# Hybrid attention and recurrent layer on one core: six gate columns as three two-column units of seven half-products in the recurrent stage, and new owners for two small jobs of the attention stage

## The chip, the cores and the metric

The kernel runs on one core of one Trainium2 chip. The metric is device time in microseconds (us); of several runs the median is told. One further execution was recorded by the hardware profiler, and all rows below come from it. The engines are PE (TensorE: matrix products and transposes), DVE (VectorE), ACT (ScalarE), POOL (GpSimd) and SP (SyncE, which here only issues transfers). Each works through its own queue in order, and waits for the others by semaphores.

## The reference, cut to what matters

One layer for 1024 prompt frames and 32 decode frames, 1056 columns in the kernel:

```python
h = _rms_norm(x, g_pre_mix)
z = h @ w_in
qa, ka, va, qb, fb, ib, ob, ga, gb = jnp.split(z, SPLIT_POINTS, axis=-1)
...
ya = _sink_attention(...)             # 16 heads of width 64, 2 kv heads
yb, s_fin = _hgrn2(qb, fb, ib, s0, lb, block)    # 8 heads of width 128
mix = jax.nn.sigmoid(ga) * (ya @ w_br_a) + jax.nn.sigmoid(gb) * (yb @ w_br_b)
x = x + _rms_norm(mix @ w_out, g_post_mix)
...                                   # ConvFFN and the per-layer input
```

Everything is float32. The two gates `ga` and `gb` are 1024 wide each: 16 gate columns of 128. They depend on `h` and `w_in` alone and are needed first in the mix, so the kernel can compute them whenever it likes before that.

## The kernel before, in words

**Products.** Activations lie transposed, 128 rows of features by frames. A float32 product is made of three products of rounded halves: every operand is split into a high part (a copy into a rounding type) and a low part (the value less the high part), and `product` (L195) issues high x high (L200), high x low (L201) and low x high (L202). The frames are three groups `GR` of 384, 384 and 288 columns. A weight column of 128 outputs has eight blocks of 128 inputs, so a plain column is 3 groups x 8 blocks x 3 = 72 products: 48 on 384 columns and 24 on 288. `La`, `Lb` are the high and low parts of `h`.

**Weights.** `plan` lists the weight columns in the order of their use. `load_raw` (L168) issues the load on SP into one of two `wr` buffers. `load_next` (L173) makes the two halves in the eight `wb` buffers: the high half on ACT (L181) or, from position 28 of the attention stage on, on DVE (L183, switched by `hi_on`), the low half on DVE (L184). `next_w` keeps two columns ahead of the one in use.

**Attention stage** (L841 to L875). `stream` (L256) runs 18 plain columns as blocks of 24 products (one group of one column), two halves of 12 each: eight q columns (the first begun earlier), eight columns of `ga` and three of `gb` (`GB_AT`). After each half it runs small jobs listed for that position. For each of eight pairs of heads i and nine tiles of frames j these are `scores` (four products on PE, L451 and L452; addition of the bias and minimum on DVE, L457; exp on ACT, L462; reciprocal and two scalings on DVE, L464 and L466; the sink's column on POOL, L455), `turn` (four transposes on PE, L478; high half `ph` on ACT, L223; low half `pl` on DVE, L224) and `values` (products on PE, L500 and L501; two copies on ACT, L507; two additions on DVE, L509). `turn` stands three halves behind `scores`, `values` two behind `turn`. The gates' products are there because the small jobs load DVE and ACT more than PE. `h_sums` (L514) makes sums of quarters of `h` on DVE, for the next stage, and stores them through POOL's queue (L528, to `t_d`); `ya` is stored when a pair is done.

**Recurrent stage** (L878 to L1318). One more plain gate column bridges the change of stage. Then the 32 columns of q, f, i and og run as 16 units of two columns. A unit (`unit_pieces`, L991) computes the 384-column groups 0 and 1 of two columns together in the seven block products of Strassen's scheme (Winograd's form): seven pieces of 12 products on 384 columns, in place of eight. Group 2 stays plain, four pieces of 12 on 288 columns. Operands are quarters of `h` or their sums (`TH`, `TL`, loaded from `t_d` at L885, split by `t_split` at L887), and quarters of the weights or their sums (`b_parts`, L922: eight splits, L931 on ACT and L932 on DVE, and four sums on DVE, L933 to L944). The bias of the scheme is settled in the evictions e0 to e10: copies on ACT, additions on DVE. In between run the small jobs of the recurrence (decay, factors, turns, `tile_in`, `tile_out`, `group_out`). After head 7 the last four gate columns follow as plain blocks: `tail[:8]` still beside head 7's jobs, `tail[8:]` beside `load_split` of `ya` (L1337: load on SP into `ld`, split into `Ra` on ACT and `Rb` on DVE), which feeds the next stage's products (`Ra`, L1379).

**Order.** PE, DVE and ACT queues are ordered by the framework's scheduler from the program above; `pinned`, `step` and `behind` fix a few jobs. Each queue is then executed in order.

## Time and profile before

| what | value |
|---|---|
| median of 3 runs | 2001.58 us (2001.55 to 2002.27) |
| the profiled execution's own time | 2002.58 us |
| its span, first to last instruction | 2000.8 us |
| PE busy | 1984.3 us (99%) |
| DVE, ACT, POOL busy | 71%, 48%, 11% |
| attention stage, scores of the first pair to the last values | 56.5 to 372.8 us |
| recurrent stage with the tail, to the first product on `Ra` | 385.8 to 871.6 us |

The profiled execution is 1.00 us above the median; its time is 1.78 us more than its span. A row of a group gives line, engine, operation, output and inputs, form and count, then the busy time and the mean of one in ns, then the idle time of the engine just before and what ended it. A matmul's duration in a row contains its fill and drain, and overlaps with the next one; the pace of matmuls is the distance of their starts. Instructions on DVE and ACT overlap a little as well, so the busy time of a stretch is less than the sum of its durations.

### The profile page before, as it was taken

What the parts mean: (1) busy time and instruction counts of PE and PEld (TensorE: products, weight loads), DVE (VectorE), ACT (ScalarE), POOL (GpSimd) and SP (SyncE); (2) the same over time, 40 slices, a digit from 0 to 9 for tenths busy, and PEclk for the clock granted to TensorE, in tenths of its full rate; (3) what the DMA queues carried; (4) which work ended last, traced back from release to release, by engine and by line L of the source; (5) the groups of instructions that cost most, each with busy time, mean ns of one, the idle gap of its engine ahead of it and who ended that gap; (6) DMA issues with size and microseconds to landing.
All of it is one profiled execution on the core that took longest, in us unless ns stands there. A gap on an engine that the chain in (4) does not pass through costs nothing.

```text
span 2000.8 us, 37359 instructions
## 1 busy us (share of the span) xinstructions
PE 1984.3 (99%) x14304; PEld 1955.0 (98%) x14304; DVE 1424.5 (71%) x3138; ACT 965.4 (48%) x2159; POOL 228.4 (11%) x323
## 2 busy tenths in 40 slices
PE   8999999999999999999999999999999999999998
PEld 7899999999999999999999999999999999999998
DVE  6788888688888888554455788788888784655552
ACT  7555566566666666442124663333333344444432
POOL 1110100000000000002001023333333210000000
PEclk9999999999999999999999999999999999999999
DMA  7622311411111111377558582222222245655543
GB/s 257 155 92 85 106 53 55 154 43 58 58 37 51 41 54 54 123 241 220 166 165 291 173 288 70 80 76 86 76 86 76 86 141 195 213 192 173 171 130 80
DMA packets 253639, 247.47 MB, mean 124 GB/s; under 512 B 13893, under 2 KB 221912, under 8 KB 253461
## 3 DMA queue, kind: packets, MB, share of 16 engines
q1 hardware_dynamic: 245141, 218.59, 35.3%
q0 software_dynamic: 8240, 26.44, 3.7%
q8 instruction: 112, 1.84, 0.4%
q14 instruction: 66, 0.54, 0.1%
q10 hardware_dynamic: 80, 0.07, 0.0%
HBM read 177.56 MB, written 65.32 MB: 121 GB/s over the span
## 4 chain that ended last, share of the span: by engine, by line
PE 92%; DVE 4%; ACT 2%; DMA 1%; issue 1%; POOL 0%; SPq 0%; DVEq 0%; ACTq 0%; POOLq 0%
PE mm L200 14%; PE mm L201 14%; PE mm L202 14%; PE st L1867 7%; PE st L1866 7%; PE st L1865 7%; PE G L1009 2%; PE Y L1006 2%; PE G L1008 2%; PE G L1006 2%; PE Y L1009 2%; PE Y L1008 2%; PE tr L478 1%; PE X L1006 1%; PE so L1200 1%; PE X L1009 1%
## 5 line engine op out<-in xcount | busy, mean ns | idle before, releaser
L1865 PE MATMUL st<-op,wt 128*128 128x264 f32 x1232 | 348.6, 283 | 2.0 <-DVE Sp L1878 1.3
L1867 PE MATMUL st<-op,wt 128*128 128x264 f32 x1232 | 349.8, 284 | 0.0
L1866 PE MATMUL st<-op,wt 128*128 128x264 f32 x1232 | 347.6, 282 | 0.0
L184 DVE TENSOR_TENSOR wl<-wr,wh 128x1024 fp32r<-128x1024 f32 x129 | 157.9, 1224 | 120.7 <-ACT wh L181 111.7
L1865 PEld LDWEIGHTS st<-op,wt 128*128 128x128 f32 x1232 | 231.2, 188 | 3.5 <-DVE Sp L1878 1.7
L1866 PEld LDWEIGHTS st<-op,wt 128*128 128x128 f32 x1232 | 231.4, 188 | 0.0
L1867 PEld LDWEIGHTS st<-op,wt 128*128 128x128 f32 x1232 | 230.9, 187 | 0.0
L181 ACT CAST wh<-wr 128x1024 fp32r<-128x1024 f32 x116 | 121.8, 1050 | 197.7 <-PE mm L201 136.1
L200 PE MATMUL mm<-La,wh 128*128 128x384 f32 (+1 forms) x528 | 174.4, 331 | 0.0
L201 PE MATMUL mm<-Lb,wh 128*128 128x384 f32 (+1 forms) x528 | 170.9, 324 | 0.6 <-DVE Lb L710 0.6
L200 PE MATMUL mm<-ac,wh 128*128 128x352 f32 x528 | 170.8, 323 | 0.0
L202 PE MATMUL mm<-La,wl 128*128 128x384 f32 (+1 forms) x528 | 170.5, 323 | 0.2 <-DVE wl L685 0.2
L202 PE MATMUL mm<-ac,wl 128*128 128x352 f32 x528 | 169.8, 322 | 0.0
L201 PE MATMUL mm<-ac,wh 128*128 128x352 f32 x528 | 169.3, 321 | 0.0
L1625 ACT CAST wt<-wu 128x512 fp32r<-128x512 f32 x126 | 77.9, 619 | 186.6 <-POOL ab L1851 88.3
L200 PE MATMUL mm<-Ra,wh 128*128 128x264 f32 x512 | 145.4, 284 | 0.0
L201 PE MATMUL mm<-Rb,wh 128*128 128x264 f32 x512 | 145.0, 283 | 0.0
L202 PE MATMUL mm<-Ra,wl 128*128 128x264 f32 x512 | 145.0, 283 | 0.0
L1626 DVE TENSOR_TENSOR wt<-wu,wt 128x512 fp32r<-128x512 f32 x126 | 103.0, 820 | 39.0 <-ACT wt L1625 39.0
L462 ACT ACTIVATE sc<-sc,st 128x257 f32<-128x257 f32 (+1 forms) x144 | 69.7, 485 | 74.0 <-DVE st L457 73.0
L201 PEld LDWEIGHTS mm<-Lb,wh 128*128 128x128 f32 x528 | 99.4, 188 | 1.7 <-DVE Lb L710 1.4
L202 PEld LDWEIGHTS mm<-La,wl 128*128 128x128 f32 x528 | 99.2, 188 | 0.7 <-DVE wl L685 0.5
(496 smaller groups left out, 5694.8 us busy)
## 6 DMA issues: line engine op xcount, KB each, us to landing
wr<-in_w_down_dram SPq DMA_DIRECT2D x66, 512.0 KB
wu<-in_w_up_dram SPq DMA_DIRECT2D x42, 512.0 KB
wu<-in_w_in_dram SPq DMA_DIRECT2D x32, 512.0 KB
wr<-in_w_in_dram SPq DMA_DIRECT2D x25, 512.0 KB
ac<-act_d SPq DMA_DIRECT2D x66, 176.0 KB
act_d<-Up SPq DMA_DIRECT2D x21, 528.0 KB
wr<-in_w_out_dram SPq DMA_DIRECT2D x16, 512.0 KB
pw_d<-pw POOLq DMA_DIRECT2D x11, 512.0 KB, 5.6
```

Source lines behind the costliest of these rows:

```text
L181: S.copy(hi[:], raw[:])
L184: V.tensor_tensor(lo[:], raw[:], hi[:].bitcast(F32), op=ALU.subtract)
L200: E.matmul(ps, wh, a, start=first and n == 0, stop=False)
L201: E.matmul(ps, wh, b, start=False, stop=False)
L202: E.matmul(ps, wl, a, start=False, stop=last and n == len(ks) - 1)
L1006: E.matmul(o, wh, x[0][k], start=first and k == 0, stop=False, skip_group_check=True)
L1008: E.matmul(o, wh, x[1][k], start=False, stop=False, skip_group_check=True)
L1009: E.matmul(o, wl, x[0][k], start=False, stop=k == 3, skip_group_check=True)
L1626: V.tensor_tensor(t[:, 1], src, t[:, 0].bitcast(F32), op=ALU.subtract)
L1865: E.matmul(o, wh, xh, start=first and k == 0, stop=False, skip_group_check=True)
L1866: E.matmul(o, wh, xl, start=False, stop=False, skip_group_check=True)
L1867: E.matmul(o, wl, xh, start=False, stop=k == 3, skip_group_check=True)
```

## The change

- **Where the gates are computed.** The 16 gate columns are one list `GATES`, all of `ga` first. The attention stage gets 21 blocks, seven columns (before: eleven), spread by `G_AT` over the eight pairs: 6, 2, 2, 2, 2, 2, 2, 3. A pair from the second to the seventh has five blocks where it had six (the fourth had nine), and the last has three where it had six. One plain column still bridges the stages. Six columns become three units of two columns in the recurrent stage, after heads 2, 5 and 7 (`gate_unit`, `G_AFTER`), each of 11 pieces. Two plain columns are left for the tail: three of their six blocks beside head 7's last jobs, three beside `load_split`.
- **Low halves of weights in attention.** From position 28 on ACT makes the high half and also writes the negated value, rounded, into the low half's tile; a transfer issued from POOL then adds the raw weight to it in place (`accum_op`).
- **Scaling.** Of the two heads of a tile DVE scales one, ACT the other.
- **Order.** `h_sums` is cut into four steps, for pairs 1, 2, 4 and 5 (before: two whole at pair 0, two at pair 3). `values` stands three halves behind `turn`. At the end `back` (which reloads a part of `h` that was overwritten) comes after the last piece in place of the third last, since the gate unit's sum `gu` lies in the same buffer. Units use the `wr` and `wb` buffers alternately, counted from the end.

```diff
+    GATES = [(ta_d[c], 5376 + c * P) for c in range(8)] + [(tb_d[c], 6400 + c * P) for c in range(8)]
+    G_AT = (6,2,2,2,2,2,2,3)
+    N_A = sum(G_AT) // 3
...
-        if hi_on[0] == "act":
-            S.copy(hi[:], raw[:])
+        S.copy(hi[:], raw[:])
+        if lo_by[0] == "vector":
+            V.tensor_tensor(lo[:], raw[:], hi[:].bitcast(F32), op=ALU.subtract)
         else:
-            V.tensor_copy(hi[:], raw[:])
-        V.tensor_tensor(lo[:], raw[:], hi[:].bitcast(F32), op=ALU.subtract)
+            S.mul(lo[:], raw[:], -1.0)
+            gdma(lo[:], raw[:], accum_op=ALU.add)
...
-            for h in range(2):
-                V.tensor_scalar(sc[:m_, h, b0:e_], sc[:m_, h, b0:e_], st[:m_, 1, h:h + 1], None,
-                                op0=ALU.mult)
+            V.tensor_scalar(sc[:m_, 0, b0:e_], sc[:m_, 0, b0:e_], st[:m_, 1, 0:1], None, op0=ALU.mult)
+            S.mul(sc[:m_, 1, b0:e_], sc[:m_, 1, b0:e_], st[:m_, 1, 1:2])
...
+        H_AT = (1, 2, 4, 5)
+        of_gates = [b for n in range(N_A) for b in unit(gate_out(GATES[n][0]))]
         for i in range(8):
             lo_ = 2 * len(blocks) if i else 0
-            blocks += unit(gate_out(ta_d[i]))
-            if i in GB_AT:
-                blocks += unit(gate_out(tb_d[GB_AT.index(i)]))
-            if i < 7:
-                blocks += unit(q_out(i + 1))
-            hi_ = 2 * len(blocks) - (6 if i == 7 else 0)
+            q = unit(q_out(i + 1)) if i < 7 else []
+            g = [of_gates.pop(0) for _ in range(G_AT[i])]
+            blocks += g + q if i == 0 else q + g
+            hi_ = 2 * len(blocks) - (4 if i == 7 else 0)
...
-                    small.setdefault(at + 5, []).append(lambda i=i, js=js: values(i, js))
+                    small.setdefault(at + 6, []).append(lambda i=i, js=js: values(i, js))
...
+    G_AFTER = {2: N_A + 1, 5: N_A + 3, 7: N_A + 5}
+    BU, unit_at = [], {}
     for h in range(8):
+        unit_at[h] = len(BU)
         BU += [(1280 + h * P, 2304 + h * P), (3328 + h * P, 4352 + h * P)]
+        if h in G_AFTER:
+            BU.append(tuple(GATES[G_AFTER[h] + a][1] for a in range(2)))
...
-        cb = lp.tile([P, T], F32, tag="Lb10", name="cb")
+        cb_gu = lp.tile([P, T + GMAX], F32, tag="Lb10", name="cb")
+        cb, gu = cb_gu[:, 0:T], cb_gu[:, T:T + GMAX]
...
+        def gate_unit(h):
+            def out(dst):
+                def f(g, src):
+                    o, n = GR[g]
+                    t = gtile()
+                    S.activation(t[:, :n], src, AF.Tanh, scale=0.5)
+                    dma(dst[:, o:o + n], t[:, :n])
+                return f
+            a, b = (out(GATES[G_AFTER[h] + i][0]) for i in range(2))
+            return unit_pieces(unit_at[h] + 2, lambda: gu, a,
+                               lambda g: bt("x0", GMAX, 1)[:], b)
...
             pieces += qf_unit(h) + io_unit(h)
             m1 = m0 + NP
+            if h in G_AFTER:
+                pieces += gate_unit(h)
...
-        at(len(pieces) - 3, back)
+        at(len(pieces) - 1, back)
...
-        for c in range(4, 8):
-            u = unit(gate_out(tb_d[c]))
-            tail += [u[0], u[2], u[1]]
-        stream(tail[:8], {m - len(pieces): f for m, f in small.items()})
+        u, v = (unit(gate_out(dst)) for dst, _ in GATES[14:])
+        tail = [u[0], u[2], v[0], v[2], u[1], v[1]]
+        stream(tail[:3], {m - len(pieces): f for m, f in small.items()})
...
-        stream(tail[8:], small)
+        stream(tail[3:], small)
```

What the scheduler makes of it on ACT, a stretch inside one pair of the attention stage, before (`sc` are scores, `st` their statistics, `ph` a turned high half, `gt` a gate, `u` and `o` values, `qa` and `qb` queries):

```order
L462 ACTIVATE sc_3258,st_3259<-sc_3258,st_3259 128x257 x2
L292 ACTIVATE gt_3280<-mm_3234 128x384
L507 COPY u_3288<-o_3283 64x32
L508 COPY u_3288<-o_3283 64x32
L223 CAST ph_3294<-tr_3296 128x256
L223 CAST ph_3314<-tr_3316 128x512
L462 ACTIVATE sc_3328,st_3329<-sc_3328,st_3329 128x257
L292 ACTIVATE gt_3350<-mm_3301 128x288
L462 ACTIVATE sc_3328,st_3329<-sc_3328,st_3329 128x257
```

and the same engine in a pair of the changed kernel that makes two weight columns:

```order
L465 ACTIVATE sc_2701,st_2702<-sc_2701,st_2702 128x257 x2
L182 CAST wh_2920<-wr_2918 128x1024
L469 ACTIVATE sc_2701<-sc_2701,st_2702 128x256
L413 ACTIVATE qa_2723<-mm_2663 64x288
L226 CAST ph_2731<-tr_2733 128x512
L465 ACTIVATE sc_2745,st_2746<-sc_2745,st_2746 128x257
L416 ACTIVATE qb_2724<-mm_2663 64x288
L465 ACTIVATE sc_2745,st_2746<-sc_2745,st_2746 128x257
L226 CAST ph_2768<-tr_2770 128x512
L186 ACTIVATE wl_2921<-wr_2918 128x1024
L469 ACTIVATE sc_2745<-sc_2745,st_2746 128x256
```

New in ACT's queue are the cast of the high half (L182), the negated copy (L186) and, behind each tile's two exps, the scaling (L469), which needs DVE's reciprocal of what these exps have summed.

At the end of the attention stage SP's queue reads before:

```order
L293 DMA tb_d_111<-gt_5014 128x384
L512 DMA ya_d_92<-ya_4194 128x1056
L293 DMA tb_d_111<-gt_5067 128x288
L885 DMA TL_5076<-t_d_128 128x1536
L885 DMA TL_5079<-t_d_129 128x1536
```

and now:

```order
L514 DMA ya_d_92<-ya_3970 128x1056
L296 DMA ta_d_108<-gt_4803 128x384
L896 DMA TL_4725<-t_d_128 128x1536
L896 DMA TL_4728<-t_d_129 128x1536
```

The loads of the sums of `h` still stand behind the store of the last `ya` and one store of a gate. On PE, though, the last values product is now followed by 7 products on 384 columns and 24 on 288 before the recurrent stage's first pieces; before, it was 48 on 384 and 35 on 288.

At the end of the recurrent stage SP's queue reads now (the stores `yb_d` are head 7's last outputs, `ld` the loads that feed `Ra`):

```order
L1288 DMA yb_d_100<-sg_10334 128x384
L296 DMA tb_d_115<-gt_10828 128x288
L1288 DMA yb_d_100<-sg_10259 128x384
L296 DMA tb_d_116<-gt_10868 128x384
L1288 DMA yb_d_100<-sg_10349 128x288
L1370 DMA ld_10906<-ya_d_85 128x264
L1370 DMA ld_10910<-ya_d_86 128x264
```

As before, the first load stands right behind the last output of head 7. On PE that output's transposes were followed by 72 products on 384 columns and 24 on 288 before the first product on `Ra`; now it is 48 and 24.

More of the change, by code (lines that the diff above doesn't have):

```diff
@@ L860, in layer_kernel @@
                     small.setdefault(m, []).append(lambda: pinned(load_next, S, V))
[L861 removed]
+                small.setdefault(28, []).append(lambda: lo_by.__setitem__(0, "dma"))
             if i < 7:
                 small.setdefault(lo_ + 2, []).insert(0, lambda i=i: bias_load(i + 1))
[L864 to L865 removed]
+            if i in H_AT:
+                sums = h_sums(H_AT.index(i))
+                next(sums)
+                for m in range(4):
+                    small.setdefault(lo_ + 2 * m + 1, []).append(
+                        lambda sums=sums: pinned(lambda: next(sums), V))
             for j in range(9):
```

49 lines of the change are left out of this document (25 added, 24 removed).

## The prediction

> **What bounds the kernel now.** I read the page first: the shares of the engines, then the chain of waits.
>
> ```profile
> span 2000.8 us, 37359 instructions
> PE 1984.3 (99%) x14304; PEld 1955.0 (98%) x14304; DVE 1424.5 (71%) x3138; ACT 965.4 (48%) x2159; POOL 228.4 (11%) x323
> PE 92%; DVE 4%; ACT 2%; DMA 1%; issue 1%; POOL 0%; SPq 0%; DVEq 0%; ACTq 0%; POOLq 0%
> ```
>
> PE is busy nearly throughout and owns 92% of the chain. "Busy" may hide a PE that only creeps, so next I read starts, at a place with nothing but products (the timeline of PE):
>
> ```profile
> 864.21 0.29 PE L200 MATMUL G<-La,wh 128*128 128x288 f32 x1
> 867.39 0.34 PE L200 MATMUL X<-La,wh 128*128 128x384 f32 x1
> 871.56 0.28 PE L200 MATMUL mm<-Ra,wh 128*128 128x264 f32 x1
> 871.92 0.29 PE L200 MATMUL mm<-Ra,wh 128*128 128x264 f32 x1
> ```
>
> Between the first two starts lie 24 products on 288 columns: 3.18/24 = 0.1325 us each. Between the second and the third lie 24 on 384: 4.17/24 = 0.174 us. Three on 264 take 0.36 us. Then the stages that the change touches, in windows: the second, the sixth and the last pair of heads of the attention stage, and one head of the recurrent stage (54.74 us):
>
> ```profile
> core 0: us, PE busy (x) PEld busy (x) DVE busy (x) ACT busy (x) POOL busy (x), PEclk, DMA share, GB/s
> 115.10:149.00 33.90, 33.90 (x239) 33.67 (x237) 29.81 (x95) 20.10 (x63) 4.22 (x16) 1.00 0.29 95
> 266.60:301.90 35.30, 35.30 (x250) 34.80 (x249) 29.09 (x94) 21.11 (x66) 2.35 (x13) 1.00 0.21 69
> 337.30:372.80 35.50, 34.64 (x245) 33.32 (x244) 25.01 (x90) 20.93 (x67) 1.58 (x8) 1.00 0.12 42
> 500.00:554.74 54.74, 54.74 (x362) 53.19 (x362) 46.50 (x132) 34.68 (x93) 0.00 (x0) 1.00 0.18 53
> ```
>
> PE has no idle time in three of these, at a granted clock of 1.00. The sixth pair has six blocks, two columns: 2 x (48 x 0.174 + 24 x 0.1325) = 23.1 us of its 35.3 us. The other 12.2 us are the small jobs' own products and transposes. So PE bounds both stages, and only fewer products, or a new wait, move the time.
>
> **The saving.** Three units compute six columns with seven block products where eight stood, on groups 0 and 1: three pieces of 12 products on 384 columns fewer, 36 x 0.174 = **6.25 us**. All other products of the gates are only moved. In the recurrent stage a gate unit takes PE 84 x 0.174 + 48 x 0.1325 = 21.0 us and brings DVE eight splits, four sums and five evictions:
>
> ```profile
> L932 DVE TENSOR_TENSOR wt<-wu,wt 128x512 fp32r<-128x512 f32 x12 | 8.1, 685 | 1.8 <-ACT wt L931 1.7
> L1027 DVE TENSOR_TENSOR x<-s1c,Y 128x384 f32<-128x384 f32 x1 | 0.6, 554 | 0.3 <-PE Y L1009 0.3
> ```
>
> 12 x 0.685 + 5 x 0.554 = 11.0 us, 52% of 21.0, where a head has 46.5/54.74 = 85%. The unit thins DVE's load, and PE covers it. I count it at nothing; without that cover it would cost up to 11 us a unit. It also follows head 7, where DVE is crowded; the row of PE's idle time there,
>
> ```profile
> L1232 PE MATMUL so<-vk,am 128*128 128x128 f32 x16 | 3.3, 287 | 0.5 <-DVE S L1210 0.5
> ```
>
> is a wait for DVE that the plain tail could not avoid. With the start's delay I put it at 0.7 us and take it as gone (bounds 0 and 0.7): **-0.7 us**.
>
> **Attention, ACT and DVE.** A pair loses one block of six, on average 23.1/6 = 3.9 us, so PE needs 31.4 us. ACT's additions, by these rows of the pair at 266.6 (the first from the page):
>
> ```profile
> L181 ACT CAST wh<-wr 128x1024 fp32r<-128x1024 f32 x116 | 121.8, 1050 | 197.7 <-PE mm L201 136.1
> L462 ACT ACTIVATE sc<-sc,st 128x257 f32<-128x257 f32 x14 | 7.1, 507 | 6.6 <-DVE st L457 6.6
> L223 ACT CAST ph<-tr 128x256 fp32r<-128x256 f32 x1 | 0.4, 373 | 0.0
> ```
>
> The trace has no scaling on ACT. Its nearest rows are 0.373 us (a cast of as many columns) and 0.507 us (an exp with a per-row scale and a sum); I take 0.42, since there is no sum: nine make 3.8 us (3.4 to 4.6). A weight column costs two passes, 2 x 1.05 = 2.1 us; by the new order of ACT the third, fourth and sixth pairs make two columns, the second and fifth one, the seventh none. ACT goes from 21.1 us to 21.1 - 0.45 (a gate's tanh) + 3.8 + 4.2 = 28.65 us of 31.4 (91%) in the heavy pairs, 26.5 or 24.4 in the others. DVE by rows of the same pair:
>
> ```profile
> L184 DVE TENSOR_TENSOR wl<-wr,wh 128x1024 fp32r<-128x1024 f32 x3 | 3.7, 1226 | 0.2
> L183 DVE CAST wh<-wr 128x1024 fp32r<-128x1024 f32 x2 | 1.4, 688 | 0.0
> L466 DVE TENSOR_SCALAR sc<-sc,st 128x256 f32<-128x256 f32 x14 | 4.3, 348 | 0.2
> L520 DVE TENSOR_TENSOR hs<-La,Lb 128x384 f32<-128x384 f32 x16 | 8.1, 546 | 0.0
> ```
>
> 29.1 - 3.7 - 1.4 - 4.3/2 = 21.9 us, and in four pairs eight steps of `h_sums`, 8 x 0.546 = 4.4 us: 26.3 of 31.4 (84%). So no engine has more work than PE. The last pair is the tightest: PE 35.5 - 11.6 = 23.9 us, DVE 25.0 - 2.2 = 22.8, ACT 20.9 - 1.4 + 3.8 = 23.3; what lags there is covered by the 11.6 us of the bridging column, into which the order spreads the last turns and values. DVE at 88% cost PE nothing in the row of the pair at 115.1. ACT at 91% has no precedent in this trace, and each scaling waits for a reciprocal on DVE that waits for the exps just ahead of it; behind a waiting ACT stand casts for which DVE and then PE wait. The waits of the pair at 266.6:
>
> ```profile
> ACT sc L462 <- DVE st L457: 9.0, 9, 2.4
> DVE st L464 <- ACT sc L462: 3.0, 5, 0.7
> ```
>
> Now it is ACT that waits for DVE; with ACT late that wait shrinks, and DVE's grows. Per scaling I bound the added wait by 0 (another job stands between, as it mostly does in the order) and 0.75 us (the longest such wait here, 0.7, and a little). At 0.3 us ACT is just level with PE in the heavy pairs: 28.65 + 9 x 0.3 = 31.35. I take a value below that, with some roughness: **+1.0 us** for the stage (0 to 15.7, worked out below).
>
> **The accumulating transfers.** Nothing of this kind is in the trace. The nearest rows are POOL's transfers:
>
> ```profile
> t_d<-hs POOLq DMA_DIRECT2D x16, 192.0 KB, 2.3
> pw_d<-pw POOLq DMA_DIRECT2D x11, 512.0 KB, 5.6
> ```
>
> In the new order at least 245 instructions of PE lie between ACT's negated copy and the first product that reads the low half; at 250 in 35.3 us (the row at 266.6) that is 34 us. 5.6 us, and three times that, are hidden. In POOL's queue the transfer waits for ACT's copy, and behind it stand the sink columns (L455) of the next tiles, which the exps need; 18 or more instructions of ACT lie between. I count nothing for it.
>
> The Trainium skill speaks against this. SBUF — State Buffer, section "SBUF: two separate sides", says that transfers issued from GpSimd have their descriptors written by GpSimd, which is locked out while DVE copies float32 in a two-port mode; its section on the bandwidth-pool intuition gives 3.1 us for a transfer of 0.62 us under such copies. By that factor 5.6 us would become an estimated 28 us, still under 34 us. The trace does not bear it out so far, since 192 KB landed in 2.3 us in a stage with float32 casts on DVE; a longer lock is the fourth case below.
>
> **From attention to recurrence.** The first sums of `h` are loaded when the last `ya` is stored, split, and read by the third piece (Y):
>
> ```profile
> 372.49 0.27 PE L501 MATMUL o<-pl,Vs 32*128 32x64 f32 x1
> 374.46 0.41 ACT L292 ACTIVATE gt<-mm 128x288 f32<-128x288 f32 x1 [1.23 <-PE mm L202]
> 380.00 1.57 ACT L890 CAST TH<-TL 128x768 fp32r<-128x768 f32 x2 [0.81 <-DMA TL<-t_d]
> L885 SPq DMA_DIRECT2D TL<-t_d x4: 319/321/542, 375.5 to 376.9; - x4
> L891 DVE TENSOR_TENSOR TL<-TL,TH x8: 951/956/959, 380.9 to 395.9; 128x768 fp32r<-128x768 f32 x8
> L1006 PE MATMUL Y<-TH,wt x4: 334/334/340, 389.5 to 391.0; 128*128 128x384 f32 x4
> ```
>
> From the last values product (372.7) to the loads 2.8 us, to the two halves split 380.9 + 2 x 0.956 = 382.8: 10.1 us. PE reached Y at 389.5, 6.7 us later. Now PE has 7 and 24 products and the pieces X and G in between: 19 x 0.174 + 36 x 0.1325 = 8.1 us. The same chain is late by 2.0 us for the whole tile, by 1.0 for its first half (381.8): **+1.5 us** (0 to 4).
>
> **From recurrence to the mix.** The loads that feed `Ra` start behind head 7's last output:
>
> ```profile
> 855.27 0.55 PE L1255 MATMUL tr<-ident,vk 128*128 128x128 f32 x3
> L1340 SPq DMA_DIRECT2D ld<-ya_d x32: 319/382/1052, 856.8 to 876.4; - x32
> L224 DVE TENSOR_TENSOR Rb<-ld,Ra x32: 424/427/436, 862.3 to 879.7; 128x264 fp32r<-128x264 f32 x32
> L200 PE MATMUL mm<-Ra,wh x38: 281/282/290, 871.6 to 885.0; 128*128 128x264 f32 x38
> ```
>
> PE now has one block of 384 less in between, 24 x 0.174 = 4.2 us. On the old scale the first product on `Ra` would stand at 867.4 and the last of 32 triples at 867.4 + 31 x 0.36 = 878.6; its split ends at 879.7 + 0.4 = 880.1. **+1.5 us** (0 to 4.2).
>
> `back` moves nearer to its use: eight loads of 192 KB stand before the block that reads them by four blocks, 48 x 0.174 + 48 x 0.1325 = 14.7 us. The 32 loads of 132 KB above took 23.3 us with their splits, 0.18 MB a us; 1.5 MB takes some 8.4 us. I count nothing; without that cover it would be 8 us.
>
> **The sum.** -6.25 - 0.7 + 1.0 + 1.5 + 1.5 = -2.95 us. 2002.58 for the profiled execution becomes 1999.6, and with the 1.0 us by which the runs' median lies lower, **1998.6 us**.
>
> **The rivals.**
>
> 1. *The full saving.* Loads and splits start earlier than their old distance (the last pair has less ahead of it), and ACT's order hides the scalings: -6.25 - 0.7 + 0.5 = -6.4, **1995.2 us**. For it: no engine above 91%. Against it: both changes of stage lose cover by count.
> 2. *ACT becomes the bound of attention* (the slower side). At 0.75 us of wait per scaling a heavy pair takes 28.65 + 6.75 = 35.4 us, 4.0 over PE's 31.4, and one with one column 33.25, 1.85 over: 3 x 4.0 + 2 x 1.85 = 15.7 us. -6.25 - 0.7 + 3 + 15.7 = +11.7, **2013 us**. It decides against the change from 0.58 us a scaling on (8 us in the stage). For it: exp, reciprocal and scaling now cross between two engines above 80%. Against it: the casts and gates between them.
> 3. *The products are gone, but DVE holds the gate units back*: 12 splits and sums fall where head 7 crowds DVE, and 6 us come back: **2001 us**. Against it: 52% of load.
> 4. *Low halves come late*: at 40 us a transfer, 6 us for each of nine columns, **2052 us**. Against it: the rows of POOL above.
>
> **How the numbers follow.** The forecast 0.46, rival 1 0.28, rival 2 0.18, rival 3 0.05, rival 4 0.03. The forecast's own range, from the bounds of its terms, is 1995.5 to 2004. To leave out no more than 2 in 10 the range reaches to the full saving below and two thirds of the way to rival 2 above: **1994.5 to 2008 us**. About 0.2% (4.0 us) is what a measurement can tell from no change. Faster by more: rival 1 and 0.05 of the forecast, 0.33. Slower by more: 0.17 of rival 2, rival 4 and 0.02 of the forecast, 0.22. Within: the rest of the forecast (0.39), rival 3 and 0.01 of rival 2, 0.45.
>
> **What would show it.** The saving: 36 products on 384 columns fewer. Attention: windows of a pair at 31.4 us, ACT near 28.7 busy; PE idle there, ended by ACT's casts, would be rival 2, and waits for low halves rival 4. Recurrence: PE's idle time before the first Y and in the first triples on `Ra`, each near 1.5 us. I am wrong if either stage has more than 5 us of new idle time, or if both waits are absent.

## The result, and the profile after

| | kernel before | changed kernel |
|---|---|---|
| median | 2001.62 us (2001.55 to 2002.78, 7 runs) | 2007.43 us (2006.59 to 2009.11, 7 runs) |
| ratio, with its 95% interval | 1 | 1.0029 (1.0017 to 1.0040) |
| span of the profiled execution | 2000.8 us | 2005.7 us |

The change costs 5.8 us where 3 us of gain were forecast. The page of the changed kernel, its span, busy engines and chain of waits:

```profile
span 2005.7 us, 37309 instructions
...
PE 1980.9 (99%) x14268; PEld 1948.5 (97%) x14268; DVE 1413.5 (70%) x3089; ACT 1023.8 (51%) x2274; POOL 236.5 (12%) x332
...
PE 88%; DVE 5%; ACT 4%; issue 1%; DMA 1%; SPq 0%; POOL 0%; DVEq 0%; ACTq 0%; POOLq 0%
```

PE has 14304 - 14268 = 36 instructions fewer and is busy 3.4 us less, but its share of the chain fell from 92% to 88%: DVE and ACT now stand where PE stood. The chain says who, the windows say where. Three pairs of heads of the attention stage and one head of the recurrent stage, in the columns that the prediction shows (length, then busy time of PE, PEld, DVE, ACT, POOL):

```profile
146.50:178.90 32.40, 31.38 (x228) 30.82 (x225) 26.94 (x89) 26.98 (x78) 5.47 (x18) 1.00 0.31 93
178.90:211.10 32.20, 31.32 (x226) 30.77 (x225) 23.27 (x80) 27.26 (x77) 4.13 (x15) 1.00 0.48 126
211.10:245.00 33.90, 32.49 (x228) 31.91 (x226) 27.54 (x90) 27.57 (x78) 6.49 (x19) 1.00 0.44 118
...
500.00:554.74 54.74, 54.74 (x362) 53.40 (x361) 36.67 (x97) 25.46 (x74) 0.00 (x0) 1.00 0.24 72
```

The recurrent stage is full, at the same clock. In the attention stage PE misses 0.9 to 1.4 us of each pair, although no engine beside it is busy more than 27.6 us of 32.2 to 33.9. So this is not an engine with too much work; it is something that comes late. The waits of PE name it, first in the kernel before (115 to 373 us: one wait in all), then in the changed kernel (115 to 350 us, the largest):

```profile
PE tr L478 <- DVE pl L224: 0.7, 1, 0.7
```

```profile
PE o L502 <- DVE ya L512: 5.3, 7, 1.4
```

The products of `values` wait for the additions that read the previous result from the one `o` bank of PSUM. By form, 4.9 of these 5.3 us fall on tile 8 (the decode frames), once in each of the third to seventh pair; its values stand one half block behind those of tiles 6 and 7. That hand-over, between the last product of tiles 6 and 7 and the first one of tile 8, in the third pair of the kernel before (timeline; start, duration):

```profile
155.55 0.28 PE L501 MATMUL o<-pl,Vs 128*128 128x256 f32 x1
...
155.92 0.37 ACT L507 COPY u<-o 64x256 f32<-64x256 f32 x1 [0.24 <-PE o L501]
156.30 0.36 ACT L508 COPY u<-o 64x256 f32<-64x256 f32 x1
...
156.86 0.41 DVE L509 TENSOR_TENSOR ya<-o,u 64x256 f32<-64x256 f32 x1
...
157.28 0.43 DVE L510 TENSOR_TENSOR ya<-o,u 64x256 f32<-64x256 f32 x1
...
158.22 0.19 PE L500 MATMUL o<-ph,Vs 128*128 128x64 f32 x1
```

From the end of the products (155.83) to the end of the additions (157.71) it takes 1.88 us, and PE arrives at 158.22, 0.51 us later. In the fifth pair of the changed kernel:

```profile
221.17 0.28 PE L503 MATMUL o<-pl,Vs 128*128 128x256 f32 x1
...
222.04 0.50 ACT L465 ACTIVATE sc<-sc,st 128x257 f32<-128x257 f32 x1
...
222.45 0.19 ACT L465 ACTIVATION_READ_ACCUMULATOR sc<-sc,st 128x1 f32 x1
...
222.66 0.37 ACT L509 COPY u<-o 64x256 f32<-64x256 f32 x1
...
222.96 0.51 ACT L469 ACTIVATE sc<-sc,st 128x256 f32<-128x256 f32 x1
...
223.49 0.49 ACT L416 ACTIVATE qb<-mm 64x384 fp32r<-64x384 f32 x1
...
224.01 0.36 ACT L510 COPY u<-o 64x256 f32<-64x256 f32 x1
...
224.59 0.41 DVE L511 TENSOR_TENSOR ya<-o,u 64x256 f32<-64x256 f32 x1
...
225.01 0.43 DVE L512 TENSOR_TENSOR ya<-o,u 64x256 f32<-64x256 f32 x1
...
225.59 0.27 PE L502 MATMUL o<-ph,Vs 128*128 128x64 f32 x1 [1.41 <-DVE ya L512]
```

The same four instructions now take 4.0 us (221.45 to 225.44). The first copy waits behind other jobs of ACT, the last of them an exp, and between the two copies stand the new scaling (L469) and a piece of the next head's queries (L416). The product of tile 8 was the next in PE's order, and PE stood 1.41 us.

Read in the same way, the pairs from the third to the seventh agree. In the kernel before the hand-over takes 1.88 us in the third, fourth, sixth and seventh pair, with 0.51 to 0.53 us to spare, and 2.17 us in the fifth, with 3.3 us to spare. In the changed kernel it takes 2.98 to 3.99 us in these five pairs, and PE waits in all of them: 5.7 us of lost time, by the reckoning that follows.

To see all of it, I take for each matmul the distance from its start to the next start, less the median of that distance for the same line and width in the kernel before, and sum it by stretch. That is PE's lost time. Its level depends on how the products are grouped, the differences between kernels hardly do:

| stretch | before | change | difference |
|---|---|---|---|
| attention, first pair | 4.48 | 6.05 | +1.6 |
| attention, second to seventh pair | 1.12 | 7.04 | +5.9 |
| attention, last pair to its last values | 1.82 | 3.63 | +1.8 |
| first pieces of the recurrent stage, to the first Y | 0.00 | 0.85 | +0.85 |
| the rest of the recurrent stage and the tail | 11.15 | 10.83 | -0.3 |
| first 32 triples on `Ra` | 0.02 | 1.59 | +1.6 |

Everything else together differs by -0.6 us. The sum is +10.8; with the 6.25 us of products that are gone, +4.6 us of the spans' +4.9.

### The profile page after: what moved, and what is told of

Read it like the earlier page. It is cut to its first block, busy times and chain, and to the rows that moved or that the text cites. A ratio compares the mean times of both kernels' runs of the same rounds, so it can differ in the third digit from the quotient of the medians.

```text
span 2005.7 us, 37309 instructions
## 1 busy us (share of the span) xinstructions
PE 1980.9 (99%) x14268; PEld 1948.5 (97%) x14268; DVE 1413.5 (70%) x3089; ACT 1023.8 (51%) x2274; POOL 236.5 (12%) x332
## 4 chain that ended last, share of the span: by engine, by line
PE 88%; DVE 5%; ACT 4%; issue 1%; DMA 1%; SPq 0%; POOL 0%; DVEq 0%; ACTq 0%; POOLq 0%
PE mm L203 12%; PE mm L204 12%; PE mm L205 12%; PE st L1897 7%; PE st L1896 7%; PE st L1895 7%; PE Y L1024 2%; PE G L1024 2%; PE G L1027 2%; PE Y L1026 2%; PE Y L1027 2%; PE G L1026 2%; PE X L1024 1%; PE X L1027 1%; PE X L1026 1%
## 5 line engine op out<-in xcount | busy, mean ns | idle before, releaser
L182 ACT CAST wh<-wr 128x1024 fp32r<-128x1024 f32 x123 | 129.1, 1049 | 186.4 <-PE mm L204 125.9
L184 DVE TENSOR_TENSOR wl<-wr,wh 128x1024 fp32r<-128x1024 f32 x114 | 139.6, 1225 | 113.1 <-ACT wh L182 103.6
L203 PE MATMUL mm<-La,wh 128*128 128x384 f32 (+1 forms) x432 | 141.7, 329 | 0.4 <-ACT gt L295 0.4
L204 PE MATMUL mm<-Lb,wh 128*128 128x384 f32 (+1 forms) x432 | 140.1, 325 | 0.6 <-DVE Lb L717 0.6
L205 PE MATMUL mm<-La,wl 128*128 128x384 f32 (+1 forms) x432 | 139.9, 324 | 0.1
L205 PEld LDWEIGHTS mm<-ac,wl 128*128 128x128 f32 x528 | 99.4, 188 | 0.0
L204 PEld LDWEIGHTS mm<-ac,wh 128*128 128x128 f32 x528 | 99.2, 188 | 0.0
L203 PEld LDWEIGHTS mm<-ac,wh 128*128 128x128 f32 x528 | 99.0, 188 | 0.0
```

The costliest lines, as they stand in the source:

```text
L182: S.copy(hi[:], raw[:])
L184: V.tensor_tensor(lo[:], raw[:], hi[:].bitcast(F32), op=ALU.subtract)
L203: E.matmul(ps, wh, a, start=first and n == 0, stop=False)
L204: E.matmul(ps, wh, b, start=False, stop=False)
L205: E.matmul(ps, wl, a, start=False, stop=last and n == len(ks) - 1)
```

## The experiments

Each kernel was timed beside the kernel before, whose median lay between 2001.4 and 2001.7 us. "Lost, 2nd to 7th" is PE's lost time in these six pairs, 1.12 us before and 7.04 in the change; it comes from one profiled execution, which for e4 was its slowest (2007.88 us).

| kernel | median us | lost, 2nd to 7th |
|---|---|---|
| e1 tile 8's values one half later | 2006.64 | 5.46 |
| e2 scaling back on DVE | 2003.06 | 4.45 |
| e3 halves of weights back on DVE | 2005.20 | 5.67 |
| e4 both back (no relief; order and distances of the change) | 2005.31 | 5.87 |
| e5 e1 and e2 together | 2002.77 | 2.95 |
| e6 whole pipeline one half deeper | 2004.53 | 2.57 |
| e7 before, scaling on ACT | 2003.79 | 1.62 |
| e8 deeper, scaling on DVE | 2002.12 | 3.76 |
| e9 two units, no relief | 2006.24 | 5.25 |
| e10 deeper, no relief | 2002.13 | 4.17 |
| e11 e8 with the sums in the first pair | 1998.93 | 1.10 |
| e12 e11 with two tail blocks exchanged | 1999.31 | 1.15 |
| e13 before, values at 6 | 2006.69 | 4.90 |
| e14 change, values at 5 | 2006.84 | 6.51 |
| e15 two units, values at 5 | 2004.78 | 4.93 |
| e16 e11 without the transfers | 2001.86 | 2.44 |
| e17 change, order and place as before | 2014.17 | 10.47 |
| e18 change, order as before | 2010.73 | 11.15 |

### Is it the one `o` bank? (e1)

```diff
-small.setdefault(at + 6, []).append(lambda i=i, js=js: values(i, js))
+small.setdefault(at + 6 + (j == 8), []).append(lambda i=i, js=js: values(i, js))
```

> The change with one number altered: the values product of tile 8 is placed one half block later (7 behind its scores instead of 6), so that 24 instead of 12 block products stand between it and the values product of tiles 6 and 7, which uses the same single `o` bank. Theory T (turnaround of the one `o` bank: two copies on ScalarE and two additions on VectorE must fit into one half block of 2.1 us, and ScalarE's longer queue makes them miss it): the 0.9 to 1.6 us stops before that product in the third to seventh pair go, 7.0 us of idle TensorE time falls to under 2, and the time comes to about 2001.5 us (2000 to 2003). Theory Q (ScalarE's queue holds TensorE wherever it next needs a result, so the stop only moves): the idle time stays within 2 us of the change's, and the time is 2006 to 2009.

2006.64 us: only 0.8 us less. PE's largest waits between 115 and 350 us:

```profile
PE tr L480 <- DVE st L467: 3.6, 4, 1.4
PE s L454 <- DVE st L460: 0.8, 1, 0.8
...
PE o L502 <- DVE ya L512: 0.6, 3, 0.2
```

The 5.3 us of waits for the bank fell to 0.6, and 3.6 us appeared at the transposes of the next tiles, which wait for the scaled scores. In four of these five pairs, the third to the seventh, the additions now end 1.1 to 1.6 us before PE comes for the bank. So the bank is where the lateness shows first, and more room at this one place does not cure it. My first theory fell.

### Which relief, if any, made ACT late? (e2, e3, e4, e7)

e2, and the same edit the other way round on the kernel before (e7):

```diff
-S.mul(sc[:m_, 1, b0:e_], sc[:m_, 1, b0:e_], st[:m_, 1, 1:2])
+V.tensor_scalar(sc[:m_, 1, b0:e_], sc[:m_, 1, b0:e_], st[:m_, 1, 1:2], None, op0=ALU.mult)
```

e3 (e4 has this edit and that of e2):

```diff
-        S.copy(hi[:], raw[:])
         if lo_by[0] == "vector":
-            V.tensor_tensor(lo[:], raw[:], hi[:].bitcast(F32), op=ALU.subtract)
+            S.copy(hi[:], raw[:])
         else:
-            S.mul(lo[:], raw[:], -1.0)
-            gdma(lo[:], raw[:], accum_op=ALU.add)
+            V.tensor_copy(hi[:], raw[:])
+        V.tensor_tensor(lo[:], raw[:], hi[:].bitcast(F32), op=ALU.subtract)
```

> The change with the second head's scaling back on VectorE, the accumulating transfers kept. It takes 9 x 0.51 = 4.6 us per pair from ScalarE and gives VectorE about 9 x 0.28 = 2.5 us. If the scaling is what makes the `o` bank's copies late (T and Q alike), the stops before tile 8's values fall from 1.3 to under 0.5 us each and the time to about 2002.5 us (2001 to 2004). If ScalarE's copies of the weights are what makes them late, it stays at 2006 to 2008. If VectorE is the tighter engine (it then has some 29 us of work in 32), its own queue holds TensorE and the time is above 2008.

> The change with the weights' halves back on VectorE as before (no accumulating transfers, no copies of weights on ScalarE from the second pair on); the scaling stays on ScalarE. It takes two copies of 1.05 us per column, some 3.5 us per pair, from ScalarE and gives VectorE as many casts and subtractions, about 3.8 us per pair. If the weight copies of 1 us in ScalarE's queue make the `o` bank's copies late, the time falls to about 2002 to 2004 us; if the scaling does, it stays within 1.5 us of 2007.4; if VectorE holds TensorE, above 2009.

> The change without either relief: scaling and both halves of the weights on VectorE as before, so only the six columns are moved. VectorE has then about 26.3 + 2.5 + 3.8 = 32.6 us of work for 31.4 us of TensorE's in a pair, more than one pair holds. If that bound decides, the attention stage grows by over 1.2 us in each of six pairs beside the change's, and the time is 2010 to 2020 us. If the stops come from ScalarE's queue alone, the time is 2000 to 2003.

> The kernel before with one part of the change alone: the second head's scaling on ScalarE, everything else as before (no column moved, halves of the weights on VectorE). If the scaling costs only where the columns that covered it are gone, pairs of 35 us with 3 gate blocks still cover it, and the time is within 1 us of the kernel before, but for the first pair, where ScalarE has the halves of the weights as well: plus 0 to 1.6 us there. If the scaling on ScalarE costs by itself, it is 4 to 5 us more, as in the changed kernel.

With the changed kernel these are four corners:

| | scaling on ACT | scaling on DVE |
|---|---|---|
| low halves by transfers | 2007.43 (change) | 2003.06 (e2) |
| halves of weights on DVE | 2005.20 (e3) | 2005.31 (e4) |

The two reliefs work against each other. Each puts work on ACT. The transfers alone gain 2.2 us (e4 to e2), the scaling alone nothing (e4 to e3), and the scaling on top of the transfers costs 4.4. Of these, 1.6 us lie in the first pair: e2 loses there as little as the kernel before. In e2 the waits for the bank are half of what they were:

```profile
PE o L502 <- DVE ya L512: 2.7, 7, 0.7
```

e3 lies between its two expectations: the weight copies make up a part of the loss, not all. In the kernel before, the scaling on ACT costs 2.3 us (e7), 1.0 of it in the first pair (lost time 4.48 to 5.51), where ACT makes weight halves too; that is near what was expected if pairs of 35 us cover it (up to 1 us, and 0 to 1.6 more in the first pair), and not the 4 to 5 us expected if the scaling costs by itself. e4 was to settle whether DVE's throughput is the bound without relief; at 2005.3 it falls between the two expectations, with 5.9 us lost. So even without new work on ACT the change loses most of what it loses. e4 keeps the change's distance of `values`, order of blocks and places of `h_sums`, so it does not show the moved columns alone.

### Latency or throughput? (e5, e6, e8, e10)

e6; e8 has the scaling on DVE in addition, e10 both halves of the weights as well, and e5 is e1 and e2 together:

```diff
-small.setdefault(at + 3, []).append(lambda i=i, j=j: turn(i, j))
+small.setdefault(at + 4, []).append(lambda i=i, j=j: turn(i, j))
...
-small.setdefault(at + 6, []).append(lambda i=i, js=js: values(i, js))
+small.setdefault(at + 7 + (j == 8), []).append(lambda i=i, js=js: values(i, js))
```

> The change with both of the earlier edits that helped: the second head's scaling on VectorE and tile 8's values one half block later (24 products behind the last use of the `o` bank). The scaling on VectorE left 2.7 us of waits on the `o` bank in the third to eighth pair. Theory T (turnaround of the one `o` bank, once ScalarE's queue is short): these 2.7 us go, and the time is about 2000.5 us (1999.5 to 2001.5), under the kernel before. Theory Q (the stop moves to the next result that is awaited): 2002.3 to 2003.5.

> The change, with both reliefs kept, and every step of the attention pipeline one half block later: the transposes 4 behind their scores instead of 3, the values 7 instead of 6, tile 8's values 8. If the stops are latency (a chain over VectorE and ScalarE whose queues have work ahead of it, while both engines are idle 10 to 25 per cent of the time), one half block of 3 us more per step covers it: the 5 to 7 us of idle time go, and the time is 2000.5 to 2002.5 us. If they are throughput (ScalarE's queue fills faster than it empties), they come back at the later place: 2005 to 2008.

> The deeper pipeline with the scaling on VectorE as well. By latency both remedies serve the same stops, so they do not add up: 2000 to 2001.5 us, at most 0.7 us under the better of the two alone. If VectorE's throughput is short with the scaling back (28.8 us of 31.4), 2002 to 2004.

> All six columns moved, neither relief (scaling and halves of the weights on VectorE), and the attention pipeline one half block deeper. VectorE has 28 to 30.6 us of work in pairs of 31.2 us of products. If what was left there was latency, depth serves: 2001 to 2002.5 us. If VectorE has no room (by its load in the pairs with the sums of the state's rows, 30 us and more), depth gives nothing: 2004 to 2006, and the low halves on the transfer queue are worth their 2 to 3 us.

One half block more of distance gives 2.9 us (e6), with the same work on every engine. In the six pairs 4.5 of the 5.9 us come back, so there it is mostly latency; but the last pair loses 1.8 us more, and 2004.53 lies between the two ranges expected. The hand-overs of tile 8 take about as long as in the change (2.4 to 4.0 us in the third to seventh pair); PE comes later and finds them done, with 1.2 to 2.2 us to spare. By the medians the depth gives 3.2 us to the kernel without reliefs (e4 to e10), as expected for latency, though DVE had up to 30.6 us of work in a pair of e4. It gives only 0.9 us with the scaling on DVE and the transfers kept (e2 to e8), and e8 lies in the range that was expected if DVE's throughput is short. With the depth, the transfers are worth nothing (e8 and e10 are equal), and the scaling on ACT still costs 2.4 us (e6 against e8). e5's median is 0.3 us under e2's, in the range expected if the stop only moves, and its 11 runs spread from 2000.95 to 2006.91; it decides nothing. What is left in e8 is uneven. Two neighbouring pairs of it (windows, columns as above) and PE's largest wait between 115 and 350 us:

```profile
143.10:175.00 31.90, 31.37 (x228) 30.79 (x226) 29.07 (x97) 24.27 (x69) 6.67 (x19) 1.00 0.35 90
175.00:206.00 31.00, 31.00 (x226) 30.65 (x225) 24.97 (x89) 22.81 (x67) 3.35 (x14) 1.00 0.37 109
```

```profile
PE s L454 <- DVE st L460: 2.2, 4, 0.6
```

The first of the two is a pair with a round of `h_sums`: DVE busy 29.1 of 31.9 us and PE idle 0.5. The second has none: DVE 25.0 us, PE idle 0.0. Lost time by pair says the same: 0.9, 1.4 and 1.1 us in the third, fifth and sixth, which have sums, at most 0.2 in the fourth and seventh, which have none; only the second has sums and loses 0.05. The wait is for the addition of the bias on DVE, which frees a score bank.

### The sums of `h`, and a kernel that beats both (e11, e12, e16)

e11 puts all four rounds in the first pair; e12 exchanges two blocks of the tail in addition; e16 is e11 with e3's edit:

```diff
-            if i in H_AT:
-                sums = h_sums(H_AT.index(i))
+            for hk in range(4 if i == 0 else 0):
+                sums = h_sums(hk)
                 next(sums)
                 for m in range(4):
-                    small.setdefault(lo_ + 2 * m + 1, []).append(
+                    small.setdefault(6 * hk + m + 1, []).append(
...
-        tail = [u[0], u[2], v[0], v[2], u[1], v[1]]
+        tail = [u[0], u[2], v[2], v[0], u[1], v[1]]
```

> The deeper pipeline with the scaling on VectorE (2002.1 us), and the four rounds of sums (6 additions and subtractions each on VectorE, some 4 us) all in the first pair, whose 24 half blocks have room, instead of in the 2nd, 3rd, 5th and 6th. In the deeper kernel the pairs with sums have 29 to 29.7 us of VectorE's work and 0.9 to 1.5 us of stops, those without have 25 us and under 0.2. If VectorE's load is what is left, the stops of these three pairs go and 0.5 us comes back in the first: about 1999 us (1998 to 2000). If the places differ for another reason, 2001.5 to 2003.

> The same, with two of the six blocks behind the recurrent stage exchanged, so that three blocks of 384 columns instead of two and one of 288 stand between the last output of the recurrent stage and the first product on `Ra`: 24 products of 96 columns less ahead, as many more behind, about 0.9 us more cover. If the 1.3 us there is the short cover, it falls to about 0.4 us, and the time is 0.5 to 0.9 us under the kernel without the exchange, unless the outputs of the last head then wait for as much. If the casts onto `Ra` are bound by their loads instead, nothing changes (within 0.3 us).

> The best kernel so far (three units, pipeline one half block deeper, sums in the first pair, 1998.9 us), without the accumulating transfers: both halves of the weights on VectorE from the second pair on, scaling on VectorE. VectorE has then about 26 + 2.5 us in pairs of 31.2. If the transfers are worth nothing once the pipeline is deep enough (the thin kernel without them took 2002.1, the same as with them): 1998.5 to 1999.5 us. If VectorE's load sets the rest: 2000.5 to 2002.

e11 takes 1998.93 us, 0.9988 of the kernel before (0.9980 to 0.9997). It and e12 (1999.31 us, 0.9979 to 0.9997) are the versions here that are faster than both. The same two pairs of e11:

```profile
144.20:175.30 31.10, 31.10 (x227) 30.76 (x225) 25.22 (x89) 23.82 (x69) 4.17 (x15) 1.00 0.27 72
175.30:206.30 31.00, 31.00 (x227) 30.65 (x225) 25.10 (x89) 22.81 (x67) 3.38 (x14) 1.00 0.37 101
```

PE is full, and the six pairs lose 1.10 us, as in the kernel before. The first pair loses 4.21 (3.17 in e8). So what the deeper pipeline left was DVE's load in the pairs with sums. The hand-overs of tile 8 take 3.4 to 4.8 us in the third to seventh pair of e11, no less than in the change, yet PE waits at none of them. Without the transfers (e16) it is 2.9 us slower: 1.0 us more is lost in the second pair, where DVE is busy 29.3 us of 31.9, and 0.65 in the last; in the third DVE is busy 27.2 of 31.1 and PE is full. The transfers are worth having, once nothing else is late. e12's exchange did not help as expected: its median is 0.4 us above e11's, within the spread of the runs, the lost time at `Ra` went from 1.08 to 1.46 us, and a stop of 0.7 us appeared at head 7's products. The 1.1 us at `Ra` remain.

### The numbers that the prediction passed over (e9, e13, e14, e15, e17, e18)

e9 moves four columns instead of six, so that the pairs have six blocks as before, with no relief. e13 is the kernel before with the change's distance of `values`; e14 and e15 are the change and e9 with the old one; e18 puts each pair's gate blocks ahead of its query blocks again, and e17 does so with the old distance:

```diff
-    G_AT = (6,2,2,2,2,2,2,3)
+    G_AT = (6,3,3,3,3,3,3,3)
-    G_AFTER = {2: N_A + 1, 5: N_A + 3, 7: N_A + 5}
+    G_AFTER = {4: N_A + 1, 7: N_A + 3}
```

```diff
-small.setdefault(at + 5, []).append(lambda i=i, js=js: values(i, js))
+small.setdefault(at + 6, []).append(lambda i=i, js=js: values(i, js))
```

```diff
-            blocks += g + q if i == 0 else q + g
+            blocks += g + q
```

> Two units instead of three: attention gets one gate column per pair as in the kernel before (six blocks a pair), only the two extra columns of the fourth and the last pair and two of the four behind the recurrent stage are moved; scaling and halves of the weights on VectorE as before. It saves 2 x 2.08 = 4.2 us of products. If thin pairs are what costs, the stops in attention go, about 1.3 us stays at the products on `Ra`: 1998 to 1999.5 us. If the moved work costs wherever it is taken from, 2001 to 2003.

> The kernel before with one number altered: the values products 6 instead of 5 half blocks behind their scores, as in the change. Theory P (the place: behind 6 the additions that free the `o` bank stand in the queues behind the next tile's scores and casts): stops of 0.6 to 0.7 us before tile 8's values appear in each pair, and the time is 2005 to 2007 us. Theory N (thin pairs and ScalarE's work are the cause, the place is not): within 1 us of the kernel before.

> The change with the values back at 5 half blocks, all else kept. Theory P: the 5.3 us of stops before tile 8's values go; 2002 to 2004 us, if the casts of the weights' halves before them are ready (they have two half blocks, 6 us, instead of three). Theory N: within 1.5 us of the change, 2006 to 2009. If 6 was needed, the stops move to the casts `ph`: 2007 or more.

> Two units, no relief, values at 5. Theory P: of the 2006.2 us of the two-unit kernel the 3.4 us of waits on the `o` bank go: 2002 to 2003.5 us. Theory N: 2005 to 2007.

> The change with the gate blocks ahead of the query blocks in every pair, and the values at 5, both as in the kernel before; the columns moved and both reliefs kept. Theory O (the queries' evictions, early in the next pair, are what stands in front of the copies and additions that free the `o` bank): the stops before tile 8's values go and the time is 2001 to 2003.5 us. Theory D (thin pairs are short of slack whatever stands where; only a deeper pipeline serves): 2005.5 to 2008.

> The change with the gate blocks ahead of the query blocks in every pair, all else kept (values at 6). Theory O with the place of no weight in thin pairs: 2001.5 to 2004 us. Theory P and O together (each alone keeps the stops): 2005.5 to 2008, and only the kernel with both taken back is faster. Theory D: 2005.5 to 2008 in both.

e9 was to be the fastest and took 2006.24 us: pairs as thick as before, no new work on ACT, and a stop of 0.6 to 0.7 us before tile 8's values in five of the six. So thin pairs are not needed for the loss. e13 shows what is enough: **one number, 6 in place of 5, costs the kernel before 5.0 us** (2006.69). Its third pair, timeline:

```profile
158.79 0.28 PE L501 MATMUL o<-pl,Vs 128*128 128x256 f32 x1
...
159.50 0.47 ACT L292 ACTIVATE gt<-mm 128x384 f32<-128x384 f32 x1
...
159.99 0.37 ACT L507 COPY u<-o 64x256 f32<-64x256 f32 x1
...
160.37 0.36 ACT L508 COPY u<-o 64x256 f32<-64x256 f32 x1
...
160.77 0.42 DVE L509 TENSOR_TENSOR ya<-o,u 64x256 f32<-64x256 f32 x1 [0.33 <-ACT u L508]
...
161.20 0.43 DVE L510 TENSOR_TENSOR ya<-o,u 64x256 f32<-64x256 f32 x1
...
161.77 0.27 PE L500 MATMUL o<-ph,Vs 128*128 128x64 f32 x1 [0.89 <-DVE ya L510]
```

With 5 the copy started 0.09 us after the products; with 6 the products end at 159.07 and the copy stands behind a gate's tanh until 159.99. The hand-over takes 2.56 us where 1.88 fitted with 0.5 to spare.

The number alone does not explain the change, though. Taken back there it gives 0.6 us (e14), which the spread of the runs covers; one wait of 2.5 us appears in the fifth pair, and the other four stops of about 1 us shrink to 0.3 to 0.5. In e15 it gives 1.5 us, between the two expectations, with 3.4 of its 4.9 lost microseconds in one pair. Not all of these are waiting. Behind a stop of 1.32 us PE's granted clock is halved for 3.4 us (third column from the right in these windows of e15):

```profile
156.60:160.00 3.40, 2.08 (x15) 1.76 (x13) 3.03 (x13) 2.69 (x9) 0.19 (x1) 1.00 0.00 0
160.00:163.40 3.40, 3.40 (x15) 3.38 (x16) 3.03 (x7) 0.85 (x3) 0.00 (x0) 0.50 0.40 161
163.40:166.80 3.40, 3.40 (x28) 3.40 (x28) 2.25 (x7) 1.97 (x6) 0.42 (x2) 1.00 0.00 0
```

In it products on 288 columns start 0.24 us apart (160.31, 160.55, 160.79), where the rows of the prediction have 0.1325 us; half of the 3.4 us, 1.7 us, is what I estimate it to cost by itself. The profiles of e17, e18 and e4 have one such stretch each, in e4 outside the six pairs; the change and the kernel before have none in the attention stage, and e14 has none after its longer wait.

Nor is it the order of blocks: I expected the query pieces between the copies to be the cause, and with the old order the time is 3.3 us worse (e18), with old order and old distance 6.7 us worse (e17). Both are outside what any of my theories expected. That theory fell too: in these thin pairs the change's order is the faster one. The halved clock has a part in it: e17's runs have a mean granted clock of 0.996 to 0.998, the change's 0.999 to 1.000.

## Why the prediction was wrong

- **The saving, -6.25 us: right.** 36 instructions of PE fewer. From the first piece to the first product on `Ra` the time grew by 40.2 us (485.8 to 526.0); four columns more there at 11.55 us, less 6.25, are 39.95.
- **Attention, +1.0 us: the step that failed; +9.3 us measured** (lost time 7.42 to 16.72), more than the 5 us of new idle time that the prediction itself named as its sign of being wrong. It said "So no engine has more work than PE", and took its value from the sums of work. The sums were about right: ACT 28.65 us forecast for the third, fourth and sixth pair, and 27.0, 27.3 and 26.3 busy there; DVE 26.3 forecast for the pairs with sums, and 26.9, 27.5 and 26.4 busy in the third, fifth and sixth. The conclusion was wrong. PE's queue is in order, and each result has to be back after a fixed number of products. The hand-over of the `o` bank had 0.5 us to spare in most pairs of the kernel before, and in the change it takes 1.1 to 1.8 us longer than there. The prediction named the distance of `values` nowhere, which is to put it at nothing without a reason, and bounded the scaling by its wait for the reciprocal only. That wait came to 3.6 us of ACT's time from 146 to 345 us. Taking the scaling off ACT gives 4.4 us (e2); that the longer way for whatever stands behind it is the larger part of them is argued, not shown. Rival 2 had the sign, and the stage lost more than the 8 us from which it decides, but not by its mechanism: ACT was idle 15 to 19% of each of the three pairs shown. That 2007.43 us lies inside the stated range is luck: the range reaches up to 2008 us for rival 2's sake, while the forecast had the sign wrong and no term for these stops.
- **One scaling on ACT, 0.42 us: low.** By form, between 146.5 and 309.4 us, the exp, the scaling on ACT and DVE's own scaling:

```profile
L465 ACT ACTIVATE sc<-sc,st 128x257 f32<-128x257 f32 x70 | 35.4, 506 | 5.9 <-DVE st L460 5.5 <-DVE sc L468 0.2
...
L469 ACT ACTIVATE sc<-sc,st 128x256 f32<-128x256 f32 x35 | 17.5, 506 | 2.4 <-DVE st L467 2.4
...
L468 DVE TENSOR_SCALAR sc<-sc,st 128x256 f32<-128x256 f32 x35 | 12.2, 349 | 0.5
```

It takes what an exp takes; nine of this size make 4.6 us, the upper bound (a pair has seven of them and two narrower ones, 4.4 us). The relief takes 0.349 us from DVE for each 0.506 that it gives ACT. The Trainium skill, page "ScalarE: Activation LUTs", section "What ACT_TABLE_LOAD costs", has 280 ns and 0.833 ns an element for an instruction with a bias per row; an estimate by that page of the Trainium skill, 493 ns for 256 elements, is 3% under the row's 506.
- **Accumulating transfers, 0: right as far as landing goes.** Transfers of the low halves between 115 and 350 us, issue on POOL and landing:

```profile
L187 POOL DMA_DIRECT2D wl<-wr x9: 856/894/934, 117.3 to 278.8; - x9
...
DMA to landing us min/median/max: 4.5/5.2/6.9
```

PE never waits for a low half. The 28 us that the prediction estimated from figures of the Trainium skill's page "SBUF — State Buffer" (section "A bandwidth-pool intuition that's wrong (but worth ruling out)") did not show, with DVE busy 23 to 28 us of each pair beside them. Rival 4 is refuted. What the prediction left out is that their two copies of 1.05 us on ACT are long jobs in a queue that others wait behind.
- **Attention to recurrence, +1.5 us: mechanism right, size off;** 0.85 us lost up to the first Y.
- **Recurrence to the mix, +1.5 us: right,** +1.6 measured. The splits run later, as forecast, while PE starts on `Ra` at 875.1:

```profile
L227 DVE TENSOR_TENSOR Rb<-ld,Ra x32: 425/431/436, 867.8 to 887.5; 128x264 fp32r<-128x264 f32 x32
```

- **The old wait at head 7's end, -0.7 us: wrong.** Two stops of 0.58 and 0.56 us, up to 850.3 and 855.9, stand where one of 0.7 stood.
- **Gate units on DVE, `back`, 0: right.** The recurrent stage and the tail lose 0.3 us less than before; rival 3 is refuted.
- **The forecast's own range, 1995.5 to 2004, does not come out of its terms.** The bounds given sum to -6.95 and +17.65 us, which is 1994.6 to 2019.2 us by the median. The row of `h_sums` among DVE's prices is not of the pair at 266.6, which has none; the price itself, 0.546 us, is right in the changed kernel too.

What stays open: no kernel had thin pairs with the old distance and no relief, so the price of the thin pairs alone is not separated from that of the distance. The sums were moved to the first pair only in the deeper pipeline, so what this levelling gives without the depth is not shown. Of the 1.8 us more in the last pair at most 0.4 came back in any kernel with its three gate blocks, and why is not shown. Which jobs stand ahead of the hand-over was read in three of them, not in all; and why some stops are followed by a halved clock and longer ones are not is not shown.

## What to carry to other kernels

An engine with an in-order queue that is full needs its results back after a fixed number of its own instructions, so before moving work measure, for each such hand-over, how long it takes and how much is to spare, and not only whether the engines have room. Ask of every moved number in a schedule, even a 5 that becomes a 6, what then stands ahead of the short jobs that release a buffer. A relief that moves short jobs into a queue where others wait can cost more than it frees. If engines have idle time and stops remain, give the results more distance and level the load between the periods: here the two together brought the six pairs back to what the kernel before loses, and the distance without the levelling did not.

## What was not expected of the hardware

- ACT needs 506 ns to scale 128x256 by a value per row, DVE 349 ns; the exp of 257 columns with a sum takes the same 506 ns.
- An accumulating transfer of 512 KB within SBUF landed in 5.2 us (median), no slower than the plain one of the same size to `pw_d` in the kernel before (5.6 us), but each issue holds POOL for 0.89 us.
- A stop at the bank ends 0.14 to 0.15 us after the last addition (225.44 to 225.59, and so at the other stops of tile 8): the least distance of this hand-over that these traces show.
- Behind a stop of 1.3 us PE ran once at half the granted clock for 3.4 us (e15, 160.0 to 163.4), and started products on 288 columns 0.24 us apart in place of 0.1325.
